# Dilated attention and gated recurrence: matmul order changed between two heads, and value transposes moved into the next product

## The chip, the cores and the metric

The kernel runs on one core of one Trainium2 chip. The metric is the device time of one execution in microseconds (us), from launch to end, as the median of several runs. Times inside an execution come from one profiled run and are counted from its first instruction.

## The reference, cut to what matters

The program is two transformer blocks on 512 positions of width 1024, in float32. The change touches two places of it.

The first place is the dilated attention of the first block. There are three branches (window 128 and dilation 1, 512 and 4, 2048 and 16) with 16 heads of 64 each:

```python
q = (h @ w_q).reshape(b, s, N_BRANCHES, N_HEADS, HEAD_DIM)
for g, (window, dil) in enumerate(BRANCHES):
    o, l = _dilated_branch(q[:, :, g], kv[:, :, 0, g], kv[:, :, 1, g], window, dil, slopes[g])
wts = jax.nn.softmax(jnp.stack(lses, axis=0), axis=0)
o = jnp.sum(wts[..., None] * jnp.stack(outs, axis=0).astype(jnp.float32), axis=0)
```

A branch computes scores of queries and keys, adds a distance bias with a causal band, takes a softmax, and multiplies by the values. Queries, keys and values are products of normalized activations with weight matrices.

The second place is the gated recurrence (HGRN) of the second block, in two layers, for a context of 256 positions and the 512 latent positions. Within blocks of 128 positions it needs masked products of decayed keys and queries, also with 64 channels for each head.

## The kernel before, in words

Activations lie transposed: 128 channels on the partitions, positions along the free axis. A weight tile of 128x1024 is loaded by DMA (`wprep`), and split by ScalarE and VectorE into a high and a low float32r part (L277, L281). A **product** (`acc`, `mm3`, L284 to L294) is then 8 steps over the contraction, each with three matmuls (L286, L287, L288) of 128x128 against 128x512, so 24 matmuls.

`dilated_attention` (L639) goes over 8 pairs of heads. A pair's two heads have 64 channels each and lie on partitions 0 to 63 and 64 to 127 of the same tiles. `project(p)` (L651) makes nine products for a pair, in the order k, v, q with three branches each. ScalarE evacuates each from PSUM (L672, L676, L678). A value product goes to a tile `vt`, of which there is one buffer. Four TensorE transposes (L686) follow at once into a PSUM tile `pv`, and ScalarE copies that to the tile `v` (L687), which has two buffers for each branch. Product outputs `pq` and transposes `pv` both come from the PSUM tag `a` (two buffers of one bank).

`attend(p)` (L690) makes the scores. For each head and each of two kinds (kind 0 is branch 0; kind 1 is branches 1 and 2 side by side) there is a score tile S of two PSUM banks from tag `b` (two buffers), filled in four steps u of 128 queries. A step is one matmul (L710 or L712) or two (L715, L716), with a contraction of 64 partitions. In float32 each is carried out as two passes, each with its own weight load. VectorE adds the bias and finds the row minimum (L719), and ScalarE takes the exponential (L720). GpSimd copies small rows about (L725, L726, L743), VectorE scales the probabilities (L755), TensorE transposes them (L758, to `pt`, tag `b`) and multiplies by the values (L774, to `po`). L774 alternates between the two heads, whose outputs lie on different partitions of `po`.

In the second block `hgrn_pair` calls `scores` (L1006), and this calls `products` (L1014) eight times: once for the diagonal and once for each of seven levels. A call has two heads times `nb` blocks (4 for the latent, 2 for the context) of matmuls with a contraction of 64 (L1020), one PSUM bank for each head. GpSimd, VectorE and ScalarE compute the next level's operands meanwhile (L1053 to L1064), and VectorE merges a result under a mask (L1030). The latent runs it for two pairs in each of two layers, 32 calls in all. The context has queries in the first layer alone, 16 calls.

The program is written with the Tile framework. It records the instructions with their dependencies and arranges each engine's stream at compile time: of the instructions whose inputs and buffers are ready in its own model, the one earliest in program order goes first. So matmuls of `project(p + 1)` stand between the scores of `attend(p)`. On the chip each stream runs in that order and waits on semaphores.

Of the kernel before, what the change touches and what calls it, by code (L numbers as in the profile page):

```python
# [11 lines left out]
F32 = mybir.dt.float32  # L12
F32R = mybir.dt.float32r
U8 = mybir.dt.uint8
AF = mybir.ActivationFunctionType
ALU = mybir.AluOpType
# [3 lines left out]
P = 128  # L20
D = 1024
DT = D // P
L = 512
# [615 lines left out]
def dilated_attention(K, pool, HK, seg, gates, done):  # L639
    nc = K.nc  # L640
    a = K.a
    H = seg.H
# [8 lines left out]
    def project(p):  # L651
        q, k, v = [None] * 3, [None] * 3, [None] * 3
        jobs = [(kind, b) for kind in "kvq" for b in range(3)]
        pre = {}
        if p == 0:
            outs = [[K.bank("pq")] for _ in range(3)]
            lead_in(K, [seg], outs, [a["wk"][b * 8] for b in range(3)], [HK])
            pre = {("k", b): outs[b][0] for b in range(3)}
        for kind, b in jobs:
            if (kind, b) in pre:  # L660
                ps = pre[(kind, b)]
            else:
                W = K.wprep(a["w" + kind][b * 8 + p])
                ps = K.bank("pq")
                K.acc(ps, W, H if kind == "q" else HK, slice(0, L))
            if kind == "v":
                t = pool.tile([P, L], F32, tag="vt", name="vt", bufs=1)
            else:
                t = pool.tile([P, L], F32, tag=f"{kind}{b}", name=f"{kind}{b}", bufs=2)
            if b:  # L670

                nc.scalar.activation(t.rearrange("p (r j) -> p r j", r=4), by_residue(ps), AF.Copy,  # L672
                                     scale=0.125 if kind == "q" else 1.0)
            elif kind == "q":

                nc.scalar.activation(halves(t), ps.rearrange("p (i j r) -> p i r j", i=4, r=4), AF.Copy, scale=0.125)  # L676
            else:
                nc.scalar.activation(t, ps, AF.Copy)  # L678
            if kind != "v":
                (q if kind == "q" else k)[b] = t  # L680
                continue

            v[b] = pool.tile([P, 4, P], F32, tag=f"v{b}", name=f"v{b}", bufs=2)
            pt = K.bank("pv").rearrange("p (u n) -> p u n", u=4)
            for u in range(4):
                nc.tensor.transpose(pt[:, u], t[:, P * u:P * u + P], K.ident)  # L686
            nc.scalar.activation(v[b], pt, AF.Copy)  # L687
        return q, k, v

    def attend(p, q, k, v):  # L690
        nm = pool.tile([P, 2, 2, 4], F32, tag="nm", name="nm", bufs=2)
        den = pool.tile([P, 2, 2, 4], F32, tag="den", name="den", bufs=2)
        probs = []
        for hh in range(2):
            rows = slice(64 * hh, 64 * hh + 64)
            bias = pool.tile([P, 2, 256], F32, tag="bias", name="bias", bufs=2)
            nc.sync.dma_start(bias.rearrange("p a b -> p (a b)"), a["bias"][2 * p + hh])
            pr = pool.tile([P, 8, 256], F32, tag="pr", name="pr", bufs=2)
            probs.append(pr)
            for kind in range(2):  # L700
                for u in range(4):
                    if u == 0:
                        S = K.bank("ps", "b").rearrange("p (u c) -> p u c", u=4)
                    cs = slice(0, 256)
                    Su = S[:, u]
                    qs = q[1 if kind else 0][rows, 128 * u:128 * u + 128]
                    if kind == 0:
                        if u == 0:
                            cs = slice(128, 256)
                            nc.tensor.matmul(Su[:, 128:256], qs, k[0][rows, 0:128], start=True, stop=True)  # L710
                        else:
                            nc.tensor.matmul(Su, qs, k[0][rows, 128 * u - 128:128 * u + 128], start=True, stop=True)  # L712
                    else:
                        q2 = q[2][rows, 128 * u:128 * u + 128]
                        nc.tensor.matmul(Su[:, 0:128], qs, k[1][rows, 128 * u:128 * u + 128], start=True, stop=True)  # L715
                        nc.tensor.matmul(Su[:, 128:256], q2, k[2][rows, 128 * u:128 * u + 128], start=True, stop=True)  # L716
                    o = pr[:, 4 * kind + u, cs]
                    m = nm[:, kind, hh, u:u + 1]
                    nc.vector.tensor_tensor_reduce(o, Su[:, cs], bias[:, kind, cs], -1.0, 3e38, ALU.add, ALU.min, m)  # L719
                    nc.scalar.activation(o, o, AF.Exp, bias=m, scale=-1.0, accum_out=den[:, kind, hh, u:u + 1])  # L720

        other = pool.tile([P, 2, 2, 4], F32, tag="other", name="other", bufs=2)
# [4 lines left out]
        m = pool.tile([P, 2, 4], F32, tag="mj", name="mj", bufs=2)  # L727
# [18 lines left out]
        for kind in range(2):  # L746
            for u0 in (0, 2):
                ps = K.bank("pt", "b").rearrange("p (u c h n) -> p u c h n", u=2, c=2, h=2)
                pt = pool.tile([P, 2, 2, 2, P], F32, tag="pt", name="pt", bufs=2)
# [51 lines left out]
class Mixer:  # L801
# [204 lines left out]
    def scores(self, pr, pool):  # L1006


        K, nc, nb, n = self.K, self.nc, self.nb, self.n
        C, D, X, Y = (self.hg[q, pr] for q in "CDXY")  # L1010
        queries = not self.only_state
        out = None

        def products(kt, qt, h):  # L1014
            S = K.bank("ph", "b").rearrange("p (h u c) -> p h u c", h=2, u=4)[:, :, :nb]
            for hh in range(2):
                rows = slice(64 * hh, 64 * hh + 64)
                for c in range(nb):
                    cs = slice(c * P, c * P + P)
                    nc.tensor.matmul(S[:, hh, c], kt[rows, cs], qt[rows, cs], start=True, stop=True)  # L1020
            if h == 0:
                nc.scalar.activation(out, S, AF.Copy)
            elif h >= 32:
                for b in range(128 // h):
                    r, c = slice(h * b, h * b + h), slice(h * (b ^ 1), h * (b ^ 1) + h)
                    nc.scalar.activation(out[r, :, :, c], S[r, :, :, c], AF.Copy)
            else:
                mk = self.lmask[:, LEVELS.index(h), None, :].to_broadcast([P, nb, P])
                for hh in range(2):
                    nc.vector.copy_predicated(out[:, hh], mk, S[:, hh])  # L1030

        if queries:
            qh = self.hg["qh", pr]
            out = pool.tile([P, 2, nb, P], F32, tag="at", name="at", bufs=1)
            ks = pool.tile([P, n], F32, tag="ka_", name="ka_", bufs=2)
            nc.gpsimd.tensor_tensor(ks, C, D, op=ALU.add)
            products(ks, qh, 0)
            Cq = pool.tile([P, n], F32, tag="qa_", name="qa_", bufs=2)
            Dq = pool.tile([P, n], F32, tag="qd_", name="qd_", bufs=1)
            nc.vector.tensor_tensor(Cq, qh, X, op=ALU.mult)  # L1040
            nc.vector.tensor_tensor(Dq, qh, Y, op=ALU.mult)
        for h in LEVELS[::-1]:
            if queries:
                products(C, Cq, h)
            m = 4 if h < 64 else 2
            outer, inner = (slice(0, 4, 3), slice(1, 3)) if m == 4 else (slice(0, 1), slice(1, 2))
            view = lambda t, w, hs: t.rearrange("p (g m h) -> p g m h", m=m, h=hs)[:, :, w]
            g = n // (m * h)
            each = lambda t, w: view(t, w, 1).to_broadcast([P, g, m // 2, h])

            def widen(eng, c, d, x, tag):
                r = pool.tile([P, n], F32, tag=tag, name=tag, bufs=2)
                eng.tensor_tensor(view(r, outer, h), view(c, outer, h), each(x, inner), op=ALU.mult)  # L1053
                nc.scalar.activation(view(r, inner, h), view(d, inner, h), AF.Copy)
                eng.tensor_tensor(view(d, inner, h), view(c, inner, h), each(x, outer), op=ALU.mult)
                return r

            C = widen(nc.gpsimd, C, D, X, "ka_")
            if queries:
                Cq = widen(nc.vector, Cq, Dq, Y, "qa_")  # L1060
            nX, nY = (pool.tile([P, n // (2 * h)], F32, tag=f"{t}{h}", name=t, bufs=1 if h < 64 else 2) for t in ("tx", "ty"))
            pairs = lambda t: t.rearrange("p (g m) -> p g m", m=m // 2)
            for t, p, q in ((nX, X, Y), (nY, Y, X)):
                nc.vector.tensor_tensor(pairs(t), view(p, outer, 1)[:, :, :, 0], view(q, inner, 1)[:, :, :, 0], op=ALU.mult)  # L1064
            X, Y = nX, nY
        return out, (C, D), (Dq, Cq) if queries else None, (Y, X)
# [598 lines left out]
```

## Time and profile before

| what | value |
|---|---|
| three runs | 3463.47, 3465.73, 3468.40 us; median 3465.73 |
| profiled execution | 3466.14 us, of which 3464.0 us between first and last instruction |
| TensorE matmuls busy | 3251.7 us (94%) |
| VectorE busy | 2192.0 us (63%) |
| ScalarE busy | 1439.6 us (42%) |
| GpSimd busy | 335.1 us (10%) |
| granted TensorE clock, mean | 0.98 |

How to read it: matmuls are pipelined and their ends are modelled, so a matmul's listed duration is longer than the distance to the next one's start. Distances between starts tell what a matmul costs. The attention of the first block runs from about 590 to 1210 us, the recurrence between 1630 and 1950 us (first layer) and between 2680 and 2830 us (second).

### The profile page before, as it was taken

How to read it: one execution, taken by the hardware profiler on the slowest of the kernel's cores; microseconds unless marked ns; L12 is line 12 of the kernel's file. 1: busy time of each engine (PE TensorE's matmuls, PEld its weight loads, DVE VectorE, ACT ScalarE, POOL GpSimd, SP SyncE). 2: the span in 40 equal slices, each digit the busy share in tenths (PEclk: the TensorE clock that was granted, in tenths of full speed). 3: DMA queues.
4: the chain of work that ended last, by engine and by line, in shares of the span. 5: the costliest groups of instructions: out<-in, count | busy, mean ns of one | idle time of the engine just before them, and what ended most of it. 6: DMA issues, size and time to landing. Idle time of an engine off the chain costs nothing.

```text
span 3464.0 us, 45725 instructions
## 1 busy us (share of the span) xinstructions
PE 3251.7 (94%) x17386; PEld 2692.3 (78%) x17386; DVE 2192.0 (63%) x3997; ACT 1439.6 (42%) x2680; POOL 335.1 (10%) x670
## 2 busy tenths in 40 slices
PE   4899998999999999999998999999999899999998
PEld 4677887777767778888887768888888787778887
DVE  7898646333333499946548888965446666675456
ACT  3342335334343443336535565322324644454333
POOL 3300001111111100002102101000000320000000
PEclk9999999999999999999999899999999989999999
DMA  6568422112121256522122114541122210132232
GB/s 235 191 237 311 145 94 87 70 54 93 66 75 67 74 179 205 194 91 104 53 84 83 40 56 145 199 172 58 60 72 81 68 35 31 51 107 98 97 98 80
DMA packets 125075, 375.57 MB, mean 108 GB/s; under 512 B 14004, under 2 KB 27060, under 8 KB 124856
## 3 DMA queue, kind: packets, MB, share of 16 engines
q1 hardware_dynamic: 124856, 372.65, 31.6%
q8 instruction: 137, 2.24, 0.3%
q14 instruction: 82, 0.67, 0.1%
HBM read 365.25 MB, written 7.35 MB: 108 GB/s over the span
## 4 chain that ended last, share of the span: by engine, by line
PE 42%; DVE 6%; ACT 2%; issue 2%; POOL 1%; DMA 0%; POOLq 0%; ACTq 0%; DVEq 0%
PE pu L287 5%; PE pu L288 4%; PE pu L286 4%; PE pd L286 3%; PE pd L287 3%; PE pd L288 3%; PE pS L1212 2%; PE pj L287 1%; PE pj L286 1%; PE pj L288 1%; PE pc L288 1%; PE pc L287 1%; PE pc L286 1%; PE pO L1231 1%; PE pv L902 1%
## 5 line engine op out<-in xcount | busy, mean ns | idle before, releaser
L277 ACT ACTIVATE wh<-wr 128x1024 fp32r<-128x1024 f32 (+5 forms) x521 | 488.4, 938 | 1045.4 <-PE pd L287 299.3
L281 DVE TENSOR_TENSOR wl<-wr,wh 128x1024 fp32r<-128x1024 f32 (+5 forms) x501 | 539.1, 1076 | 605.2 <-ACT wh L277 601.3
L286 PE MATMUL pu<-h_512h,wh 128*128 128x512 f32 (+1 forms) x1472 | 562.5, 382 | 7.4 <-ACT h_512h L390 6.6
L287 PE MATMUL pu<-h_512l,wh 128*128 128x512 f32 (+1 forms) x1472 | 564.4, 383 | 3.0 <-POOL h_512l L395 2.6
L288 PE MATMUL pu<-h_512h,wl 128*128 128x512 f32 (+1 forms) x1472 | 561.6, 381 | 0.0
L286 PEld LDWEIGHTS pu<-h_512h,wh 128*128 128x128 f32 x1472 | 279.5, 190 | 59.8 <-ACT h_512h L390 7.7
L287 PEld LDWEIGHTS pu<-h_512l,wh 128*128 128x128 f32 x1472 | 279.3, 190 | 57.7 <-POOL h_512l L395 4.9
L288 PEld LDWEIGHTS pu<-h_512h,wl 128*128 128x128 f32 x1472 | 279.4, 190 | 52.8
L286 PE MATMUL pd<-g_512h,wh 128*128 128x512 f32 x656 | 256.4, 392 | 4.5 <-DVE x L399 4.2
L287 PE MATMUL pd<-g_512l,wh 128*128 128x512 f32 x656 | 255.6, 390 | 0.0
L288 PE MATMUL pd<-g_512h,wl 128*128 128x512 f32 x656 | 255.2, 389 | 0.0
L399 DVE SCALAR_TENSOR_TENSOR x<-pd,mod,x 128x512 f32<-128x512 f32 x162 | 121.1, 748 | 167.9 <-PE pd L288 167.1
L310 DVE CUSTOM_DVE_ANT_0 ada<-ada,row_c 128x1024 f32<-128x1024 f32 x144 | 185.7, 1298 | 28.2 <-DMA ada<-in_ada 24.9
L286 PEld LDWEIGHTS pd<-g_512h,wh 128*128 128x128 f32 x656 | 123.0, 188 | 33.0 <-issue 4.6
L288 PEld LDWEIGHTS pd<-g_512h,wl 128*128 128x128 f32 x656 | 123.2, 188 | 25.7
L287 PEld LDWEIGHTS pd<-g_512l,wh 128*128 128x128 f32 x656 | 123.3, 188 | 25.1 <-DVE g_512l L298 0.8
L522 ACT ACTIVATE ca<-ca 128x512 f32<-128x512 f32 (+1 forms) x110 | 64.1, 583 | 127.9 <-DVE ca L511 119.2
L287 PE MATMUL pj<-h_512l,wh 128*128 128x512 f32 (+1 forms) x280 | 107.6, 385 | 3.1 <-POOL h_512l L395 2.5
L286 PE MATMUL pj<-h_512h,wh 128*128 128x512 f32 (+1 forms) x280 | 106.0, 382 | 2.7 <-ACT h_512h L390 2.0
L288 PE MATMUL pj<-h_512h,wl 128*128 128x512 f32 (+1 forms) x280 | 106.6, 382 | 1.2 <-DVE wl L281 1.2
L281 POOL TENSOR_TENSOR wl<-wr,wh 128x1024 fp32r<-128x1024 f32 (+1 forms) x20 | 47.8, 2392 | 567.5 <-ACT wh L277 543.8
L288 PE MATMUL pc<-h_256h,wl 128*128 128x256 f32 x352 | 99.6, 283 | 0.0
(1152 smaller groups left out, 7464.6 us busy)
## 6 DMA issues: line engine op xcount, KB each, us to landing
ada<-in_ada SPq DMA_DIRECT2D x192, 512.0 KB, 4.6
wr<-in_up SPq DMA_DIRECT2D x88, 512.0 KB, 3.7
wr<-in_bup SPq DMA_DIRECT2D x88, 512.0 KB, 3.5
wr<-in_in SPq DMA_DIRECT2D x36, 512.0 KB, 3.4
wr<-in_wk SPq DMA_DIRECT2D x24, 512.0 KB, 3.5
wr<-in_wv SPq DMA_DIRECT2D x24, 512.0 KB, 3.5
wr<-in_wq SPq DMA_DIRECT2D x24, 512.0 KB, 3.5
wr<-in_out SPq DMA_DIRECT2D x48, 256.0 KB, 2.6
```

The source lines that it names most:

```text
L277: nc.scalar.activation(hi[:, :n], r[:, :n], AF.Copy)
L281: (eng or nc.vector).tensor_tensor(lo[:, :n], r[:, :n], hi[:, :n], op=ALU.subtract)
L286: mm(ps, whi, hhi, start=first, stop=False)
L287: mm(ps, whi, hlo, start=False, stop=False)
L288: mm(ps, wlo, hhi, start=False, stop=last)
L310: nc.vector.tensor_tensor_reduce(o, r, cond, 1.0, 0.0, ALU.mult, ALU.add, mod[:, t:t + 1])
L399: self.nc.vector.scalar_tensor_tensor(x, ps, gate, x, op0=ALU.mult, op1=ALU.add)
L522: K.last_silu = nc.scalar.activation(ca, ca, AF.Silu)
L902: nc.tensor.matmul(ps, hh[:, s], w[0][:, ws], start=kt == 0, stop=False)
L1212: nc.tensor.matmul(S[:, o:o + m], self.q[h][rows, qs], kt[rows, :], start=True, stop=True)
L1231: nc.tensor.matmul(O[:, qb % 2 * P:qb % 2 * P + P], vals[kb], at[:, kb * P:kb * P + P], start=qb % 2 == 0 and kb == 0, stop=qb % 2 == 1 an ...
```

## The change

Three edits. In `project`, a value product is evacuated directly into the tile `v`. Its transposes are kept back until the first half (contraction steps 0 to 3) of the next product has been issued; they go to `pv` and are copied back over `v` in place. In `attend`, the loop over heads moves inward: both heads' S tiles of a kind are open together, and matmuls alternate between the heads. In `products`, the loop over heads moves inside the loop over blocks.

```diff
+        def to_tokens(b):
+            pt = K.bank("pv").rearrange("p (u n) -> p u n", u=4)
+            for u in range(4):
+                nc.tensor.transpose(pt[:, u], v[b][:, u], K.ident)
+            nc.scalar.activation(v[b], pt, AF.Copy)
...
-                K.acc(ps, W, H if kind == "q" else HK, slice(0, L))
-            if kind == "v":
-                t = pool.tile([P, L], F32, tag="vt", name="vt", bufs=1)
+                K.acc(ps, W, H if kind == "q" else HK, slice(0, L), range(4))
+                if turn is not None:
+                    to_tokens(turn)
+                    turn = None
+                K.acc(ps, W, H if kind == "q" else HK, slice(0, L), range(4, 8))
...
+            if kind == "v":
+                v[b] = t.rearrange("p (u n) -> p u n", u=4)
+                turn = b
...
+        for kind in range(2):
+            S = [K.bank("ps", "b").rearrange("p (u c) -> p u c", u=4) for _ in range(2)]
+            for u in range(4):
+                us = slice(128 * u, 128 * u + 128)
+                cs = slice(128 if kind == 0 and u == 0 else 0, 256)
+                if kind:
+                    parts = [(slice(0, 128), q[1], k[1], us), (slice(128, 256), q[2], k[2], us)]
+                else:
+                    parts = [(cs, q[0], k[0], slice(max(128 * u - 128, 0), 128 * u + 128))]
+                for to, qt, kt, ks in parts:
+                    for hh in range(2):
+                        rows = slice(64 * hh, 64 * hh + 64)
+                        nc.tensor.matmul(S[hh][:, u, to], qt[rows, us], kt[rows, ks], start=True, stop=True)
+                for hh in range(2):
+                    o = probs[hh][:, 4 * kind + u, cs]
...
         def products(kt, qt, h):
-            for hh in range(2):
-                rows = slice(64 * hh, 64 * hh + 64)
-                for c in range(nb):
-                    cs = slice(c * P, c * P + P)
+            for c in range(nb):
+                cs = slice(c * P, c * P + P)
+                for hh in range(2):
+                    rows = slice(64 * hh, 64 * hh + 64)
                     nc.tensor.matmul(S[:, hh, c], kt[rows, cs], qt[rows, cs], start=True, stop=True)
```

## Rows read from the trace of the kernel before

**Rows 1.** The page: busy time by engine; the chain that ended last, by engine.
```profile
PE 3251.7 (94%) x17386; PEld 2692.3 (78%) x17386; DVE 2192.0 (63%) x3997; ACT 1439.6 (42%) x2680; POOL 335.1 (10%) x670
PE 42%; DVE 6%; ACT 2%; issue 2%; POOL 1%; DMA 0%; POOLq 0%; ACTq 0%; DVEq 0%
```

**Rows 2.** Busy time by stretch: attention, recurrence of first and second layer.
```profile
core 0: us, PE busy (x) PEld busy (x) DVE busy (x) ACT busy (x) POOL busy (x), PEclk, DMA share, GB/s
690.00:760.00 70.00, 64.05 (x341) 48.44 (x339) 22.94 (x66) 27.96 (x58) 9.04 (x48) 1.00 0.17 60
1860.00:1900.00 40.00, 34.62 (x219) 27.73 (x219) 38.78 (x94) 20.10 (x44) 17.32 (x18) 0.91 0.14 52
2785.00:2820.00 35.00, 32.04 (x213) 27.23 (x213) 27.98 (x57) 17.59 (x40) 12.12 (x15) 0.85 0.11 38
```

**Rows 3.** Waits in 600 to 1180 us: who waited for whom, total, times, longest.
```profile
PE pv L686 <- ACT vt L672: 21.1, 15, 1.4
```

**Rows 4.** Instructions on tile pv: duration min/median/max, first and last start.
```profile
L687 ACT ACTIVATE v<-pv x24: 597/598/600, 587.7 to 1157.1; 128x512 f32<-128x512 f32 x24
```

**Rows 5.** Timeline, 28 matmuls of products in a row: start, duration, what.
```profile
689.92 0.39 PE L287 MATMUL pq<-h_512l,wh 128*128 128x512 f32 x1
...
696.26 0.39 PE L288 MATMUL pq<-h_512h,wl 128*128 128x512 f32 x1
```

**Rows 6.** Timeline at the end of a value product.
```profile
662.71 0.39 PE L288 MATMUL pq<-hk7h,wl 128*128 128x512 f32 x1
662.91 1.06 ACT L277 ACTIVATE wh<-wr 128x1024 fp32r<-128x1024 f32 x1 [3.89 <-PE pq L287]
663.87 0.58 ACT L678 ACTIVATE vt<-pq 128x512 f32<-128x512 f32 x1
664.51 0.66 PE L686 MATMUL pv<-mats,vt 128*128 128x128 f32 x4 [1.41 <-ACT vt L678]
```

**Rows 7.** Timeline, transposes inside a product with their input at hand.
```profile
715.73 0.48 PE L287 MATMUL pq<-hk1l,wh 128*128 128x512 f32 x1
716.05 0.92 PE L758 MATMUL pt<-mats,pr 128*128 128x128 f32 x7
```

**Rows 8.** Windows, instructions on pq alone, score phases of two pairs (PE, PEld, ...).
```profile
696.58:710.70 14.12, 6.46 (x17) 2.76 (x16) 0.58 (x1) 1.00 0.16 56
783.68:798.43 14.75, 6.79 (x20) 3.36 (x21) 0.00 (x0) 1.00 0.44 155
```

**Rows 9.** Timeline of a score step in steady state, and visits of one tile alone.
```profile
701.98 0.70 PE L712 MATMUL ps<-k,q 64*128 64x256 f32 x2
702.51 0.38 PE L715 MATMUL ps<-k,q 64*128 64x128 f32 x2
702.71 0.42 DVE L719 CUSTOM_DVE_ANT_0 pr<-ps,bias 128x256 f32<-128x256 f32 x1 [0.63 <-PE ps L712]
702.73 0.38 PE L716 MATMUL ps<-k,q 64*128 64x128 f32 x2
703.05 0.50 PE L288 MATMUL pq<-hk2h,wl 128*128 128x512 f32 x1
703.15 0.43 DVE L719 CUSTOM_DVE_ANT_0 pr<-ps,bias 128x256 f32<-128x256 f32 x1
703.48 0.49 PE L710 MATMUL ps<-k,q 64*128 64x128 f32 x2
703.89 0.51 PE L286 MATMUL pq<-hk3h,wh 128*128 128x512 f32 x1
...
710.09 0.48 PE L715 MATMUL ps<-k,q 64*128 64x128 f32 x2
710.41 0.38 PE L716 MATMUL ps<-k,q 64*128 64x128 f32 x2
710.72 0.50 PE L287 MATMUL pq<-hk5l,wh 128*128 128x512 f32 x1
```

**Rows 10.** Timeline, a visit that holds scores of both heads.
```profile
704.33 0.37 PE L715 MATMUL ps<-k,q 64*128 64x128 f32 x1
704.36 0.48 PE L712 MATMUL ps<-k,q 64*128 64x256 f32 x1
...
704.98 0.50 PE L287 MATMUL pq<-hk3l,wh 128*128 128x512 f32 x1
```

**Rows 11.** Timeline, value products that alternate between the heads.
```profile
719.89 2.03 PE L774 MATMUL po<-pt,v 128*64 128x128 f32 x32
721.85 1.09 PE L758 MATMUL pt<-mats,pr 128*128 128x128 f32 x8
```

**Rows 12.** Timeline, one call of products, latent and context.
```profile
1658.89 0.72 PE L1020 MATMUL ph<-qa__13133,ka__13129 64*128 64x128 f32 x8 [0.21 <-DVE qa__13133 L1053]
1659.55 0.39 PE L287 MATMUL pj<-h_256l,wh 128*128 128x256 f32 x1
...
1876.05 1.71 PE L1020 MATMUL ph<-qa__15556,ka__15552 64*128 64x128 f32 x16
1877.69 0.50 PE L287 MATMUL pj<-h_512l,wh 128*128 128x512 f32 x1
```

**Rows 13.** Windows (as rows 2), a stretch at a lower granted clock.
```profile
1940.00:1950.00 10.00, 10.00 (x38) 6.50 (x37) 5.31 (x11) 0.92 (x2) 0.06 (x1) 0.55 0.15 54
```

**Rows 14.** Chain of waits: one matmul of a product at the low clock.
```profile
1906.87 0.43 PE pj L288
```

More of the change, by code (lines that the diff above doesn't have):

```diff
@@ L664, in project @@
                 ps = K.bank("pq")
-                K.acc(ps, W, H if kind == "q" else HK, slice(0, L))
-            if kind == "v":
-                t = pool.tile([P, L], F32, tag="vt", name="vt", bufs=1)
-            else:
-                t = pool.tile([P, L], F32, tag=f"{kind}{b}", name=f"{kind}{b}", bufs=2)
+                K.acc(ps, W, H if kind == "q" else HK, slice(0, L), range(4))
+                if turn is not None:
+                    to_tokens(turn)
+                    turn = None
+                K.acc(ps, W, H if kind == "q" else HK, slice(0, L), range(4, 8))
+            t = pool.tile([P, L], F32, tag=f"{kind}{b}", name=f"{kind}{b}", bufs=2)
             if b:
@@ L678, in project @@
                 nc.scalar.activation(t, ps, AF.Copy)
-            if kind != "v":
+            if kind == "v":
+                v[b] = t.rearrange("p (u n) -> p u n", u=4)
+                turn = b
+            else:
                 (q if kind == "q" else k)[b] = t
[L681 to L687, printed above, removed]
         return q, k, v
@@ L692, in attend @@
         den = pool.tile([P, 2, 2, 4], F32, tag="den", name="den", bufs=2)
-        probs = []
+        biases, probs = [], []
         for hh in range(2):
-            rows = slice(64 * hh, 64 * hh + 64)
[L696 to L717, printed above, removed]
@@ new lines, in attend @@
+            biases.append(pool.tile([P, 2, 256], F32, tag="bias", name="bias", bufs=2))
+            nc.sync.dma_start(biases[hh].rearrange("p a b -> p (a b)"), a["bias"][2 * p + hh])
+            probs.append(pool.tile([P, 8, 256], F32, tag="pr", name="pr", bufs=2))
+        for kind in range(2):
[5 more added lines that the diff above has]
+                    parts = [(slice(0, 128), q[1], k[1], us), (slice(128, 256), q[2], k[2], us)]
+                else:
+                    parts = [(cs, q[0], k[0], slice(max(128 * u - 128, 0), 128 * u + 128))]
[5 more added lines that the diff above has]
+                    o = probs[hh][:, 4 * kind + u, cs]
@@ L718, in attend @@
                     m = nm[:, kind, hh, u:u + 1]
-                    nc.vector.tensor_tensor_reduce(o, Su[:, cs], bias[:, kind, cs], -1.0, 3e38, ALU.add, ALU.min, m)
+                    nc.vector.tensor_tensor_reduce(o, S[hh][:, u, cs], biases[hh][:, kind, cs], -1.0, 3e38,
+                                                   ALU.add, ALU.min, m)
                     nc.scalar.activation(o, o, AF.Exp, bias=m, scale=-1.0, accum_out=den[:, kind, hh, u:u + 1])
@@ L1015, in products @@
             S = K.bank("ph", "b").rearrange("p (h u c) -> p h u c", h=2, u=4)[:, :, :nb]
-            for hh in range(2):
-                rows = slice(64 * hh, 64 * hh + 64)
-                for c in range(nb):
-                    cs = slice(c * P, c * P + P)
+            for c in range(nb):
+                cs = slice(c * P, c * P + P)
+                for hh in range(2):
+                    rows = slice(64 * hh, 64 * hh + 64)
                     nc.tensor.matmul(S[:, hh, c], kt[rows, cs], qt[rows, cs], start=True, stop=True)
```

## The prediction

> **What bounds the kernel now.** I read the page first. TensorE's matmuls are busy 94% of the span, VectorE 63%, and the chain that ended last lies on PE by far the most [rows 1]. A busy PE can hide waits, so I then read the stages by windows. In the attention, 70 us hold 64 us of PE against 23 us of VectorE and 28 us of ScalarE, all at the full granted clock [rows 2]. TensorE alone sets that stage, and its time there counts one for one. In the recurrence VectorE takes 38.8 of 40 us in the first layer; in the second it takes 28.0 of 35 and PE 32.0 [rows 2]. There a shorter matmul counts in part.
>
> The list of waits then shows what TensorE waits for in the attention: transposes L686 for the evacuation of `vt` [rows 3]. The timeline gives the price. A product's matmuls start 6.34/28 = 0.226 us apart [rows 5]. The last one of a value product starts at 662.71; ScalarE first ends a weight split (1.06 us), then evacuates (0.58 us), and the transposes start at 664.51 [rows 6]: 1.80 us for a matmul worth 0.226.
>
> **Edit A, transposes inside the next product.** There are 24 of them (24 copies L687 [rows 4]), three for each of eight pairs. Now 12 matmuls of the next product follow at once, 12 x 0.226 = 2.7 us. The evacuation ended about 664.45, 1.74 us after the last matmul started [rows 6], so it fits with 1 us to spare. Breaking into a product where the input is at hand costs 0.32 us from the matmul before to the first transpose (715.73 to 716.05) [rows 7]. So 1.80 - 0.32 = 1.48 us goes, 24 times: **35.5 us**. The transposes and both ScalarE copies stay as many as before, and the way back from transposes to a product is walked once each time, before and after. No DMA moves past another: weight loads keep their order on SP's queue.
>
> What is late next? Three things could be. The copy of `pv` over `v` must end before the product after next needs the bank; it has the other 12 matmuls, 2.7 us, for 0.60 us of work [rows 4]. Weight splits, 1.06 us of ScalarE for each product [rows 6], have 24 x 0.226 = 5.4 us. The wait now stands in the middle of a product, and behind it in TensorE's stream stands that product's second half; nobody waits for that but its own evacuation. If the cover went altogether, the wait would be back, a gain of 0. The other end is 24 x (1.80 - 0.226) = 38 us, with no break at all. I take 35.5, because rows 6 and 7 are both direct measurements.
>
> **Edit B, scores alternate between heads.** The score phase of the pair at 696.58 lasts 14.12 us and holds 16 matmuls of products (17 less the one still in flight at its start) [rows 8]. These are worth 3.6 us, so the scores cost 10.5 us of TensorE. The phase of 14.75 us holds 20: 10.2 us. I take 10.3.
>
> A steady step runs from 701.98 to 703.48, 1.50 us: score matmuls of two S tiles 1.07 us (to 703.05), one matmul of a product, and two changes between 64 and 128 rows; of the 0.43 us from 703.05 to 703.48 the product is worth 0.226, so a change costs about 0.2 [rows 9]. The two S tiles are kind 0 and kind 1 of one head, on the same 64 partitions, so their passes queue up. One visit shows the alternative by chance: L715 of one head and L712 of the other start 0.03 us apart, and the visit, with six passes like the other, lasts 704.33 to 704.98, 0.65 us instead of 1.07 [rows 10]. So both halves of the array work at once, and 0.42 us of each step could go.
>
> Not all of it will. The next step of a tile starts only after VectorE has read the last one. With both heads started at s, VectorE begins 0.73 us later (701.98 to 702.71) and takes 0.44 us for each (702.71 to 703.15) [rows 9], so the first head's next step may start at s + 1.2 and the second's at s + 1.6. If the stream still holds one product matmul for each step, the steps alternate between about 1.2 (TensorE then waits for the second head) and 1.46 us (the second head, being late, leaves less to wait for): a mean of 1.33 instead of 1.50. Eight steps, the first a short one of 0.41 (703.48 to 703.89 [rows 9]) and a change of 0.2: 0.62 + 7 x (1.33 - 0.226) = 8.35 us for a pair, against 10.3. The last pair has no project behind it and its chain goes over VectorE and GpSimd, so I count seven pairs: 7 x 1.95 = **14 us**. The ends are in the rivals: 26 us gained, 18 us lost. I take the value nearest to rows 9, where VectorE's pace and the static order are those measured.
>
> By the Trainium skill (TensorEngine Tiling (Array Packing), Theoretical Speedup), a contraction of 64 or less may run up to 2 times as fast. Rows 10 bear out that the two halves run together; the sum by that rule is the second rival below.
>
> **Edit C, recurrence.** A latent call takes 1.64 us (1876.05 to 1877.69) for 16 passes [rows 12]. Head after head already overlaps a little. Where matmuls alternate, 32 passes take 1.96 us [rows 11], 0.055 for each beside a change of 0.2; 16 would take 0.88 + 0.2 = 1.1 us, a gain of 0.55. The context's call of 8 passes takes 0.66 us [rows 12] and would take 0.64: nothing. So 32 x 0.55 = 18 us of TensorE. In the first layer VectorE is full and hides it; I let a fifth through, 2 us. In the second PE and VectorE share the bound; I let half through, 4 us. Together **6 us**, bounds 0 and 18.
>
> **Sum.** 35.5 + 14 + 6 = 55.5 us off the profiled execution's own 3466.1 us gives 3410.6. That execution lay 0.4 us above the median of the runs, so 3410. Its own range is 3397 to 3426 (A 33 to 37, B 7 to 20, C 0 to 12).
>
> **Rivals.**
> - *Split steps, 3442.* VectorE frees the heads 0.44 us apart, so the compile-time order could put a product's matmul between them. Each head then comes alone: a short visit takes 0.41 us (703.48 to 703.89) and a full one of four passes 0.63 (710.09 to 710.72) [rows 9], so a pair's 16 visits with their changes cost 2 x 0.41 + 14 x 0.63 + 16 x 0.2 = 12.9 us, 2.6 more than 10.3: 7 x 2.6 = 18 us lost, 35.5 + 6 - 18 = 24 gained. Against it: two tiles freed the same 0.44 us apart already stand in one visit in rows 9.
> - *Full overlap, 3398.* With more product matmuls in each step VectorE never holds TensorE: 0.41 + 7 x 0.65 + 8 x 0.2 = 6.6 us a pair, 7 x 3.7 = 26 us; 35.5 + 26 + 6 = 67.5. For it: rows 10. Against: the order must change.
> - *The bank, 3446.* `pq` and `pv` share two buffers. If these were handed out in turn, each product after a value product would wait for the evacuation of the one before, and A would be 0: 14 + 6 = 20 gained. Against: in the second block's attention one tile holds one of two buffers while four transposes go through the other (L1223 to L1228), which handing out in turn would not allow.
> - *The clock, 3485, slower.* The stretch at 1940 has PE busy all 10 us at a granted clock of 0.55, near the lower level of 1.2 GHz [rows 13], and it is full of matmuls of 64 rows and transposes; a product's matmul then takes 0.43 us [rows 14]. If twice as dense work on 64 rows drew the clock down in the score phases, a pair would lose 16 x 0.2 = 3.3 us on products and about 4 on scores, and some 2 us more until the clock is back: 9.4 x 8 = 75 us, 55.5 - 75 = -20. It decides from 55.5/8 = 7 us a pair. Against: the clock is at full in the attention now, through idle times and scores [rows 2].
>
> **How the numbers follow.** The forecast 0.57, full overlap 0.14, split steps 0.13, the bank 0.06, the clock 0.07, and 0.03 for several small losses that cancel. The range 3388 to 3448 takes in the first two, the split and most of the bank, and a larger part of C. A measurement here can tell 0.2%, 7 us, from no change. Faster 0.90, same 0.03, slower 0.07.
>
> **What would show it.** A: no wait of L686 for an evacuation, 0.32 us from a product's matmul to the first transpose, in its middle. B: steps of about 1.33 us, both heads' matmuls a few hundredths apart or with a short wait for VectorE; visits of 0.64 us that hold one head alone would show the split. C: calls of 1.1 us, and more idle PE around them in the first layer. The prediction is wrong if products wait at their start, if the clock falls below 1.00 between 600 and 1180 us, or if the stage before 1180 us shrinks by less than 40 us.

## The result, and the profile after

| | before | after |
|---|---|---|
| median (range) of four runs each | 3465.59 us (3463.47 to 3468.40) | 3407.58 us (3404.39 to 3412.42) |
| profiled execution, span | 3466.14, 3464.0 us | 3404.39, 3402.3 us |

The ratio is 0.984, 95% interval 0.982 to 0.986: 58 us faster, at 3408 us against 3410 forecast. First the page of the changed kernel, busy time by engine as in [rows 1]; then one row of windows for each stage, of before and then of after: the attention (from its first matmul to the first of the next part) and the latent's recurrence in the second layer (from its first to its last `ph` matmul). Columns as in [rows 2].

```profile
PE 3206.1 (94%) x17386; PEld 2659.6 (78%) x17386; DVE 2186.9 (64%) x3997; ACT 1436.4 (42%) x2680; POOL 338.3 (10%) x670
```

```profile
556.20:1226.90 670.70, 614.76 (x3246) 476.28 (x3246) 261.28 (x685) 274.76 (x576) 84.79 (x394) 0.99 0.21 73
...
2758.70:2829.30 70.60, 62.32 (x440) 53.92 (x440) 55.59 (x120) 31.97 (x72) 25.47 (x31) 0.85 0.08 27
```

```profile
556.50:1177.40 620.90, 591.59 (x3246) 465.67 (x3246) 257.35 (x685) 272.93 (x576) 84.55 (x394) 0.99 0.23 78
...
2702.90:2767.60 64.70, 52.71 (x438) 43.99 (x439) 55.50 (x120) 31.69 (x72) 26.43 (x31) 0.87 0.09 30
```

With the same instructions, attention is 49.8 us shorter and the second layer 5.9. The latent's recurrence in the first layer (its row stands under edit C) is 8.0 us shorter. That makes 63.7; the stretches between give 2.0 back, and the spans differ by 61.7.

**Edit A in the trace.** The timeline around a value product, to be laid beside [rows 6]:

```profile
655.29 0.39 PE L288 MATMUL pq<-hk7h,wl 128*128 128x512 f32 x1
655.49 1.06 ACT L277 ACTIVATE wh<-wr 128x1024 fp32r<-128x1024 f32 x1 [3.90 <-PE pq L287]
655.51 0.39 PE L286 MATMUL pq<-hk0h,wh 128*128 128x512 f32 x1
...
656.45 0.58 ACT L689 ACTIVATE v<-pq 128x512 f32<-128x512 f32 x1
...
658.01 0.40 PE L288 MATMUL pq<-hk3h,wl 128*128 128x512 f32 x1
658.24 0.60 PE L665 MATMUL pv<-mats,v 128*128 128x128 f32 x4
658.60 0.48 PE L286 MATMUL pq<-hk4h,wh 128*128 128x512 f32 x1
658.94 0.60 ACT L666 ACTIVATE v<-pv 128x512 f32<-128x512 f32 x1 [1.91 <-PE pv L665]
```

The product ends at 655.29 and the next one follows 0.22 us later. ScalarE still splits first and evacuates then (to 657.03), and TensorE does not notice. The transposes begin 0.23 us after a product's matmul (1.80 in [rows 6]) and the product goes on 0.36 us after that. No wait of L665 is left in the list of waits.

**Edit B in the trace.** Score steps in steady state, as in [rows 9]; PEld is the weight load ahead of the first matmul:

```profile
689.72 0.68 PEld L718 LDWEIGHTS ps<-k,q 64*128 64x128 f32 x8 [0.25 <-DVE nm L722]
689.72 0.87 PE L718 MATMUL ps<-k,q 64*128 64x128 f32 x8
...
690.47 0.42 DVE L722 CUSTOM_DVE_ANT_0 pr<-ps,bias 128x256 f32<-128x256 f32 x1 [0.64 <-PE ps L718]
690.52 0.50 PE L288 MATMUL pq<-hk2h,wl 128*128 128x512 f32 x1
690.82 0.42 DVE L722 CUSTOM_DVE_ANT_0 pr<-ps,bias 128x256 f32<-128x256 f32 x1
...
690.96 1.05 PE L718 MATMUL ps<-k,q 64*128 64x128 f32 x8
...
692.37 0.88 PE L718 MATMUL ps<-k,q 64*128 64x128 f32 x8
...
693.61 0.37 PE L718 MATMUL ps<-k,q 64*128 64x128 f32 x1
```

Steps start 1.24, 1.41 and 1.24 us apart. The first one shown waits 0.25 us for VectorE's reading of the step before it, with one product matmul between. Between 595 and 1210 us, all visits of TensorE to the scores (from the first score matmul to the next other one, and the extra distance ahead of it) cost 80.0 us before, in 82 visits, and 63.5 after, in 66: 16.5 us saved. Five pairs went from 10.3 to 7.7 us, the last from 9.4 to 7.9; the other two, with 9.7 and 9.5 us the cheapest of the first seven before, only to 8.6.

Something came back. The list of waits, 600 to 1130 us, of before and of after:

```profile
PE pt L758 <- DVE pr L755: 9.8, 7, 1.7
```

```profile
PEld ps L718 <- DVE nm L722: 16.7, 55, 0.4
...
PE pt L762 <- DVE pr L759: 15.4, 7, 2.4
```

The lines on `pt` are TensorE standing before a pair's first probability transpose until VectorE has scaled the probabilities: 5.6 us more after, in seven pairs. (The line on `ps` sums 55 waits like the one shown above, 0.30 us on average.) Both heads' scores now end together, and the chain behind them (GpSimd's copies, the factors, the scaling) is longer: in five pairs the first probability transpose came 4.4 us after the last score before and 5.1 to 5.2 us after the change, with 11 matmuls of products beside the chain in both.

A second thing came with this wait. For the seventh pair, the first row of each fence is TensorE's wait, from the start of the matmul ahead of it, and the second is a stretch just behind; before, then after, with the granted clock in the column PEclk:

```profile
1113.70:1115.72 2.02, 0.39 (x3) 0.00 (x1) 1.54 (x11) 1.17 (x2) 0.85 (x5) 1.00 0.05 19
1117.80:1121.20 3.40, 3.39 (x37) 2.56 (x37) 3.01 (x8) 2.04 (x3) 1.40 (x7) 1.00 0.00 0
```

```profile
1066.58:1069.33 2.75, 0.39 (x2) 0.03 (x1) 1.72 (x12) 0.21 (x1) 1.40 (x9) 1.00 0.18 68
1070.70:1074.10 3.40, 3.40 (x21) 2.08 (x20) 3.01 (x10) 1.07 (x3) 1.88 (x10) 0.50 0.02 5
```

After the longer wait the granted clock fell to half (0.50). In this profile it does so behind two of the seven waits, and the pattern runs through all 14 profiles of this case. Before, five of the seven distances from a product's matmul to the first probability transpose are about 2.0 us; after, five are 2.7 to 2.8. The six profiles without edit B have the shorter waits and no time at half clock between 600 and 1160 us. The eight with it have the longer ones and two to four stretches at half clock each, eight in the kernel with the longest waits (3.9 to 4.3 us). All but one of these stretches begin 2.5 to 5.1 us after the matmul ahead of such a wait started.

**Edit C in the trace.** A latent call, beside the second pair of [rows 12], and then the latent's recurrence in the first layer from its first to its last `ph` matmul, before and after:

```profile
1824.21 1.16 PE L1024 MATMUL ph<-qa__15532,ka__15528 64*128 64x128 f32 x16
1825.30 0.50 PE L287 MATMUL pj<-h_512l,wh 128*128 128x512 f32 x1
```

```profile
1862.70:1951.60 88.90, 80.04 (x474) 63.85 (x474) 77.42 (x161) 37.03 (x81) 31.80 (x34) 0.85 0.13 47
```

```profile
1813.20:1894.10 80.90, 66.26 (x474) 52.09 (x474) 76.89 (x161) 36.96 (x81) 32.06 (x34) 0.92 0.15 51
```

The call takes 1.09 us instead of 1.64. Not every call shows this, as some wait for operands and some run at half clock: all visits of TensorE to `ph` sum to 37.0 us instead of 41.1 in the first layer and to 31.6 instead of 39.4 in the second. In the first layer, VectorE has 77 us of work in both; what differs beside TensorE's work is the granted clock, 0.85 and 0.92. Whether the 8 us are the edit's or the clock's is asked below.

### The profile page after: what moved, and what is told of

Read it like the earlier page. It is cut to its first block, busy times and chain, and to the rows that moved or that the text cites. A ratio compares the mean times of both kernels' runs of the same rounds, so it can differ in the third digit from the quotient of the medians.

```text
span 3402.3 us, 45745 instructions
## 1 busy us (share of the span) xinstructions
PE 3206.1 (94%) x17386; PEld 2659.6 (78%) x17386; DVE 2186.9 (64%) x3997; ACT 1436.4 (42%) x2680; POOL 338.3 (10%) x670
## 4 chain that ended last, share of the span: by engine, by line
PE 41%; DVE 7%; ACT 2%; issue 2%; DMA 1%; POOL 1%; SPq 0%; POOLq 0%; ACTq 0%; DVEq 0%
PE pu L287 5%; PE pu L286 5%; PE pu L288 5%; PE pd L286 3%; PE pd L287 3%; PE pd L288 3%; PE pS L1216 2%; PE pj L286 1%; PE pj L287 1%; PE pj L288 1%; PE pc L288 1%; PE pc L287 1%; PE pc L286 1%; PE pO L1235 1%; PE pv L906 1%
```

## The experiments

### Each edit by itself

Edit A alone: `project` from the changed kernel, `attend` and `products` from the one before.

```diff
...
-                K.acc(ps, W, H if kind == "q" else HK, slice(0, L))
...
+                K.acc(ps, W, H if kind == "q" else HK, slice(0, L), range(4))
+                if turn is not None:
+                    to_tokens(turn)
+                    turn = None
+                K.acc(ps, W, H if kind == "q" else HK, slice(0, L), range(4, 8))
...
```

> The kernel before with the first edit alone: value transposes in place, half a product later. Theory (TensorE stood still for the evacuation, 1.57 us for each of 24 value products): 35 to 38 us faster than before, 3428 to 3431, all of it between 600 and 1180 us, and no wait of a transpose. Rival (the wait moves to the start of the product after, which needs the shared bank): no more than 7 us faster.

Measured: 3421.59 us, ratio 0.987 (0.985 to 0.989). Attention 629.6 us against 670.7, 41 us less, so A is the main part; another 7 us went in the first layer's recurrence, which A does not touch (see the last experiment).

Edit B alone: `attend` from the changed kernel.

```diff
-        for hh in range(2):
...
-            for kind in range(2):
-                for u in range(4):
...
+        for kind in range(2):
...
+            for u in range(4):
...
+                for to, qt, kt, ks in parts:
+                    for hh in range(2):
...
```

> The kernel before with the second edit alone: scores of the dilated attention alternate between two heads. Theory (both halves of the array work at once, VectorE's reading of the tile sets the step): steps of 1.24 to 1.40 us instead of 1.50, 14 to 17 us faster, 3449 to 3452. Rival (the steps gain only because the first edit keeps products ready beside them): under 7 us faster. Rival (steps split): slower by some 18 us.

Measured: 3453.57 us, ratio 0.997 (0.996 to 0.998), 11 us, less than the 14 to 17 expected. Attention is 6.7 us shorter. The visits cost what they cost in the changed kernel, 16.5 us less than before, but the distances from a product's matmul to the probability transposes sum to 25.3 us, before 18.0. The saving in the scores is real and nearly half of it comes back as that wait. Of the 9.2 us left, 2.5 more are missing; the stage has 22.4 us at half clock in this profile, 11.9 before, and 10.5 us more at half speed are worth up to 5 us.

Edit C alone: `products` from the changed kernel.

```diff
-            for hh in range(2):
...
-                for c in range(nb):
...
+            for c in range(nb):
...
+                for hh in range(2):
...
```

> The kernel before with the third edit alone: the recurrence's products alternate between two heads. Theory (a latent call takes 1.1 instead of 1.64 us, 32 calls, and more of it gets through than the 6 us predicted, since the profile after shows 8 us in the first layer and 6 in the second): 10 to 14 us faster. Rival (these stretches start at another moment after the first two edits and meet their loads and transfers differently): 2 to 6 us.

Measured: 3460.13 us, ratio 0.998 (0.997 to 1.000), 6 us; the theory's 10 to 14 did not come. The latent's recurrence in both layers of this kernel, in windows as above:

```profile
1861.90:1951.10 89.20, 71.87 (x474) 55.24 (x474) 77.13 (x161) 36.58 (x80) 31.85 (x33) 0.87 0.14 46
...
2760.40:2825.00 64.60, 51.06 (x439) 42.60 (x439) 55.60 (x120) 31.85 (x72) 25.65 (x31) 0.89 0.09 30
```

In the second layer 64.6 us, as in the changed kernel (before: 70.6). In the first layer TensorE is busy 8.2 us less and the stage is as long as before; VectorE has its 77 us there. That VectorE hides the gain is argued, not shown. Over all 14 profiles the second layer took 64.4 to 65.2 us with the edit and 70.3 to 70.6 without. C is worth 6 us in the second layer and, by the last experiment, about 1 at most in the first.

### Why the wait of edit A was there

The kernel before with the value evacuated into `v`, which has two buffers, and the transposes in place but directly behind the product:

```diff
-                t = pool.tile([P, L], F32, tag="vt", name="vt", bufs=1)
+                t = pool.tile([P, L], F32, tag=f"v{b}", name=f"v{b}", bufs=2)
...
-            v[b] = pool.tile([P, 4, P], F32, tag=f"v{b}", name=f"v{b}", bufs=2)
+            v[b] = t.rearrange("p (u n) -> p u n", u=4)
```

> The kernel before with value products evacuated into the two-buffered tile and transposed in place, but at once, as before. Theory (the gain is the matmuls that cover the evacuation): no change, within 7 us of before, and the transposes start 1.80 us after the last matmul. Rival (the single buffer of the old tile held the evacuation up): most of the 35 us gained.

Measured: 3462.55 us, ratio 0.999 (0.998 to 1.001); the gap from the last matmul of a value product to its transposes is still 1.79 us. The single `vt` was not the reason, and the work in place by itself brings nothing.

The changed kernel, with the transposes placed after one contraction step of the next product instead of four:

```diff
-                K.acc(ps, W, H if kind == "q" else HK, slice(0, L), range(4))
+                K.acc(ps, W, H if kind == "q" else HK, slice(0, L), range(1))
...
-                K.acc(ps, W, H if kind == "q" else HK, slice(0, L), range(4, 8))
+                K.acc(ps, W, H if kind == "q" else HK, slice(0, L), range(1, 8))
```

> The changed kernel, but a value product's transposes stand after the first of the next product's eight contraction steps (3 matmuls, 0.68 us) instead of the fourth. Theory (the matmuls in between are the cover of an evacuation that ends some 1.7 us after the last matmul): each of 24 transposes again waits, about 1.80 - 0.23 - 0.68 = 0.9 us, so 21 us slower than the changed kernel, about 3429. Rival (any place inside the next product will do, since the bank or the buffer was what held TensorE): within 7 us of the changed kernel.

Measured: 3408.01 us, ratio 0.984 (0.983 to 0.985): no slower than the changed kernel, so 3429 did not come. In the timeline seven matmuls stand between the product and the transposes, though the source puts three there:

```profile
652.84 0.39 PE L288 MATMUL pq<-hk7h,wl 128*128 128x512 f32 x1
653.07 0.39 PE L286 MATMUL pq<-hk0h,wh 128*128 128x512 f32 x1
...
654.42 0.39 PE L286 MATMUL pq<-hk2h,wh 128*128 128x512 f32 x1
654.65 0.64 PE L665 MATMUL pv<-mats,v 128*128 128x128 f32 x4
```

The compile-time order moves ready matmuls ahead of transposes whose input is late. Then why not in the kernel before? There the product being evacuated holds one of the two banks of tag `a`, and `pv`, asked for ahead of the next `pq`, the other; the next product had no bank to start in. Two runs test that. The first is the kernel before with one word changed, `pv` from another tag:

```diff
-            pt = K.bank("pv").rearrange("p (u n) -> p u n", u=4)
+            pt = K.bank("pv", "s").rearrange("p (u n) -> p u n", u=4)
```

> The kernel before, with one thing changed: the transposed value product is allocated from the third kind of PSUM bank (two of them, used otherwise by the output product and the sums) instead of from the two banks that the value products themselves come from. Transposes are written where they were, directly behind the product, into a copy, with one vt buffer. Theory (it was the turn of the two banks that kept the next product's matmuls behind the transposes, and once the turn is free they are put ahead of them): the gap from the last matmul of a value product to its transposes falls from 1.80 to about 0.23 us, attention is 35 to 42 us shorter, the whole 3421 to 3430 us, which is what the projection edit alone gave. Rival (the place inside the next product that the source gives the transposes is what covers the evacuation): gap stays 1.80, whole time within 5 us of 3463 to 3466.

Measured: 3423.62 us, ratio 0.988 (0.986 to 0.990); attention 631.7 us, 2 us more than with edit A alone. Around a value product:

```profile
660.71 0.39 PE L288 MATMUL pq<-hk7h,wl 128*128 128x512 f32 x1
...
661.88 0.58 ACT L672 ACTIVATE vt<-pq 128x512 f32<-128x512 f32 x1
...
662.30 0.39 PE L286 MATMUL pq<-hk2h,wh 128*128 128x512 f32 x1
662.53 0.64 PE L686 MATMUL pv<-mats,vt 128*128 128x128 f32 x4
```

The gap is 0.23 us with seven matmuls ahead, in 23 of the 24 products (1.55 in the first), and nothing else of edit A is in this kernel. The bank was the reason. The second run is the changed kernel with the order forced: three matmuls, the transposes, then the rest.

```diff
-                K.acc(ps, W, H if kind == "q" else HK, slice(0, L), range(4))
+                K.acc(ps, W, H if kind == "q" else HK, slice(0, L), range(1))
+                pin = nullcontext()
                 if turn is not None:
-                    to_tokens(turn)
+                    pin = K.tc.issue_after(to_tokens(turn).ins)
                     turn = None
-                K.acc(ps, W, H if kind == "q" else HK, slice(0, L), range(4, 8))
+                with pin:
+                    K.acc(ps, W, H if kind == "q" else HK, slice(0, L), range(1, 8))
...
```

> The changed kernel, with the transposes held in front: the next product gives three matmuls, then the four transposes, and its other 21 matmuls are ordered behind them. Theory (TensorE stands until the evacuation of the value product is done, and each matmul put ahead of the transposes takes 0.227 us of that wait): the gap from last matmul of the product to first transpose is 1.80 us as before, with three matmuls in it, so 1.80 minus 3 x 0.227 = 1.1 us, less 0.23 for one ordinary step, are waited, about 0.9 us x 24 = 21 us: whole time 3425 to 3433 us. Rival (what cost the time was not the evacuation but the change itself between the product's matmuls and fp32 transposes): no difference, within 4 us of the changed kernel's 3405 to 3410.

Measured: 3433.98 us (3427.04 to 3447.31), ratio 0.992 (0.989 to 0.994); the median is 1 us above the expected range. Attention is 644.4 us, 23.5 more than in the changed kernel. The gap is 1.12 us in 23 of the 24 products (1.78 in the first):

```profile
665.08 0.39 PE L288 MATMUL pq<-hk0h,wl 128*128 128x512 f32 x1
665.57 0.58 ACT L685 ACTIVATE v<-pq 128x512 f32<-128x512 f32 x1
...
666.20 0.66 PE L665 MATMUL pv<-mats,v 128*128 128x128 f32 x4 [0.73 <-ACT v L685]
```

So the wait is for the evacuation, and each matmul ahead of the transposes takes its 0.227 us off it: 1.80 with none, 1.12 with three, 0.23 with seven.

### Must the matmuls alternate finely, and is more to be had?

The changed kernel with the loop over heads outside that over the parts, so that inside a step one head follows the other:

```diff
-                for to, qt, kt, ks in parts:
-                    for hh in range(2):
-                        rows = slice(64 * hh, 64 * hh + 64)
+                for hh in range(2):
+                    rows = slice(64 * hh, 64 * hh + 64)
+                    for to, qt, kt, ks in parts:
...
```

> The changed kernel, but inside a score step of kind 1 both matmuls of one head come before both of the other, instead of alternating matmul by matmul. Theory (the array takes up the other half's passes a few instructions ahead, and VectorE's reading sets the step): within 5 us of the changed kernel. Rival (halves work together only where neighbours in the stream alternate): kind 1 steps go back to 1.5 us, 7 to 10 us slower.

Measured: 3408.48 us, ratio 0.984 (0.983 to 0.986), visits 63.5 us: the same. But this does not show that the order inside a step is without effect. In all 66 visits the passes signal the other engines in the same sequence as in the changed kernel, and in 62 they start at the same distances to 0.012 us (between the two executions of the changed kernel, in 63). So the compile-time order was probably the same in both, whatever the source says, and the question is open.

One S tile for each step, with both heads in it, so that the next step does not wait for VectorE's reading of the last:

```diff
-            S = [K.bank("ps", "b").rearrange("p (u c) -> p u c", u=4) for _ in range(2)]
             for u in range(4):
+                S = K.bank("ps", "b").rearrange("p (h c) -> p h c", h=2)
...
-                        nc.tensor.matmul(S[hh][:, u, to], qt[rows, us], kt[rows, ks], start=True, stop=True)
+                        nc.tensor.matmul(S[:, hh, to], qt[rows, us], kt[rows, ks], start=True, stop=True)
...
```

> The changed kernel with one score tile for each step, both heads in a bank each, two buffers, instead of one tile for each head and kind. So a step's matmuls wait for VectorE's reading of the step before last, not of the last one. Theory (VectorE's reading holds the steps at 1.24 to 1.40 us): the wait of score matmuls for VectorE, 16.7 us in all now, goes, steps near 1.1 us, 6 to 12 us faster than the changed kernel, unless the probability transposes, which already wait for VectorE, wait longer by the same amount. Rival (the next wait takes it all): within 4 us.

Measured: 3410.88 us (3408.11 to 3419.11), ratio 0.985 (0.984 to 0.987): no gain. The visits did shrink, to 34 and 44.6 us (63.5). The wait took most of that:

```profile
PE pt L762 <- DVE pr L759: 26.8, 7, 3.9
```

The distances to the probability transposes sum to 36.5 us against 23.6, 12.9 of the 18.9 won. The profiled execution also had more of the stage at half clock, 44.9 us against 16.7; 28.2 us more at half speed are worth up to 14 us. This execution was the slowest of its four, but all four had a lower mean granted clock (0.972 to 0.978) than the changed kernel's four (0.979 to 0.982), so the clock has a part in the median as well. Here the wait at the probability transposes was the longest, 3.9 to 4.3 us of distance, and a stretch at half clock stands behind each of the seven.

The same alternation in the scores of the second block's attention (L1212 of the changed kernel):

```diff
-            for c in range(2):
...
-                S = K.bank("pS", "b")
...
-                for kt, m in keys:
-                    nc.tensor.matmul(S[:, o:o + m], self.q[h][rows, qs], kt[rows, :], start=True, stop=True)
-                    o += m
+            SS = [K.bank("pS", "b") for _ in range(2)]
...
+            for kt, m in keys:
+                for c in range(2):
...
+                    nc.tensor.matmul(SS[c][:, o:o + m], self.q[h][rows, qs], kt[rows, :], start=True, stop=True)
+                o += m
...
```

> The changed kernel, and the same alternation in the second block's attention, whose two score halves lie on partitions 0 to 63 and 64 to 127 as well. A latent query block has 8 passes, 4 of 512 and 4 of 256 columns, about 2.6 us head after head. Theory (halves run together): 1.3 us less for each of 32 latent query blocks, 41 us of TensorE; VectorE and ScalarE take part of it back, so 10 to 35 us faster than the changed kernel. Rival (that stage waits for its softmax, not for its scores): within 5 us.

Measured: 3416.65 us, ratio 0.987 (0.985 to 0.988): 9 us slower than the changed kernel, which neither theory said. The first layer's attention kept its length. The second's, from the end of the recurrence to the last score, in the changed kernel, in this one, and in the one with a tile for each step:

```profile
2767.60:2967.70 200.10, 194.96 (x1125) 153.00 (x1123) 124.60 (x220) 94.31 (x200) 13.87 (x8) 1.00 0.13 44
```

```profile
2768.00:2979.70 211.70, 206.74 (x1144) 159.94 (x1144) 128.54 (x223) 94.42 (x201) 14.36 (x8) 0.97 0.14 44
```

```profile
2775.80:2982.20 206.40, 201.29 (x1125) 156.95 (x1124) 124.60 (x220) 94.47 (x200) 13.88 (x8) 0.97 0.13 42
```

The third kernel has this stage unchanged and is 6.3 us longer there at the same 0.97. So about half of the 11.6 us may be the clock; the rest comes with the edit, and why is open. Nor did the run test its theory: in the second layer 15 of the 128 score passes start within 0.05 us of the pass before, in this kernel as in the changed one, and the visits to these scores cost 42.2 us against 40.1. (In the first block's attention, edit B took that count from 10 to 81 of 384 passes.) The alternation stands in the source, and TensorE's stream hardly shows it; what kept the halves apart is not shown.

### The first layer's 8 us

Both kernels once more, unchanged, for a second profile of each.

> The kernel before, once more, for its profile. Theory (the 7 us that the changed kernel wins in the recurrence of the first block is time at half clock, which differs from one execution to the next and has no part in the edits): the time at half clock between 1830 and 1980 us is another one than the 30.6 us of the first profile, by 3 to 20 us, and the length of the recurrence differs by half of that. Rival (the half-clock stretches are fixed by the program): 30.6 us again, within 2, and the same recurrence length within 1 us.

> The changed kernel, once more, for its profile. Theory (half-clock time of the first block's recurrence differs from execution to execution): another one than the 13.6 us of the first profile, up to 30 us, and the recurrence longer by half of the difference. Rival (fixed by the program): 13.6 us within 2, the recurrence 7 to 8 us shorter than before's again.

Measured: 3469.59 and 3410.17 us. The first layer, before and after:

```profile
1863.10:1953.50 90.40, 80.14 (x474) 63.90 (x474) 77.56 (x161) 36.95 (x81) 31.60 (x34) 0.85 0.14 46
```

```profile
1812.90:1900.90 88.00, 71.09 (x474) 54.94 (x474) 77.47 (x161) 37.19 (x81) 32.47 (x34) 0.86 0.15 47
```

The changed kernel takes 80.9 us in one execution and 88.0 in the other, at 0.92 and 0.86. The kernel before came out alike twice in clock (27.3 us at half in the stage both times) and 1.5 us apart in length; in the wider window of the expectation, 30.7 and 27.3 us. So for that kernel neither theory nor rival fits; in the changed kernel 10.2 us more at half clock go with 7.1 us more length, where the theory had half. Over all 14 profiles the stage took 80.9 to 83.2 us where at most 20.5 us of it lay at half clock, and 87.0 to 90.5 where 23.9 or more did. Edit C does not sort them: edit A alone (82.1 us, clock 0.92) is among the short ones, and C alone (89.2) among the long. At equal time at half clock, the profiles with and without edit C lie close: 80.9 us with all edits and 82.1 with A alone, at 13.7 us each; 82.9 with the early transposes and 83.2 with B alone, at 17.1. So up to 8 us of a measured difference there go with the clock of an execution, and about 1 with edit C. All four profiles with the attention's waits as before lie among the long ones; of the ten with a shorter attention six are short. Whether a shorter attention shifts these odds is open.

## Why the prediction was right, and where by luck

**Edit A**: 35.5 us forecast. By the median gaps, with the way back to the product, (1.796 + 0.41) before less (0.23 + 0.355) after, 1.62 x 24 = 38.9 us. The term that was off is the break into a product, taken as 0.32 us from [rows 7]. It measured 0.23, an ordinary step. In the rows, a transpose stands right ahead of the matmul that the 0.32 us are counted from:

```profile
715.71 0.27 PE L758 MATMUL pt<-mats,pr 128*128 128x128 f32 x1
715.73 0.48 PE L287 MATMUL pq<-hk1l,wh 128*128 128x512 f32 x1
```

So part of that transpose's time was taken for a price of the break; each of the 14 distances of 0.32 us in the trace of before has one 0.02 to 0.09 us ahead. For the rest, the reason given was half of it: the cover is as said, 1.8 us of evacuation behind matmuls, but the place of the transposes in the source does not make it. The bank did, as `pv` in another tag showed. The rival "the bank" looked for this in the kernel after; it stood in the one before.

**Edit B**: 14 us forecast. Its steps came as worked out (1.24 and 1.41 us against 1.2 and 1.46), with VectorE's reading as the limit, and the visits gave 16.5 us over eight pairs. The term that was mis-sized is what comes late next: the longer wait for the scaled probabilities, counted as nothing, measured 5.6 us. The cost of a pair was also forecast too high, 8.35 us against 7.7 in five pairs, while the two pairs that were cheap before gained about 1 us each instead of 1.95. B is worth about 11 us in the attention: 38.9 + 16.5 - 5.6 = 49.8, and the stage shrank by 49.8. That match is closer than the terms are known: by themselves, A took 41 us off the stage and B 6.7, and the clock's 2 us are in neither sum.

**Edit C**: 6 us forecast, 4 of them in the second layer and 2 in the first; 6 and about 1 at most measured. A call with its operands at hand came out at 1.09 us against 1.1. The visits fell by 12 us in all, against 18 forecast. Of TensorE's 9.6 us less in the second layer, 5.9 went through.

**The rivals.** Split steps and full overlap did not come; the steps alternate as forecast. The clock came, small: in the attention the granted clock fell below 1.00, which the prediction had named as a sign that it would be wrong. 16.7 us lay at half speed instead of 11.9 (23.5 in the second profile, with a stage of 624.3 us, 3.4 longer for 6.8 more at half). That is 2 to 6 us, not 75. Nor did it come where the rival put it, in the score phases with their dense work on 64 rows: it fell behind the wait for the probabilities, which edit B made longer. The profiles sort by that wait; no run changed the wait alone, so that it is the cause is not shown. The rival's 2 us until the clock is back rest on no row; a stretch of 3.4 us at half clock costs up to 1.7.

**The sum**: 49.8 + 6 = 55.8 us from the edits against 55.5 forecast. A was 3 too small and B 3 too large, so part of that closeness is luck. The other 6 us between the two profiled executions are the first layer's 8.0, most of which go with the clock, less the 2.0 given back between the stages.

## What to carry to other kernels

Where TensorE waits for an evacuation, look at what holds the next work's buffer: an order made at compile time fills the wait by itself as soon as the next product can have a bank, so ask for that bank first or take the short-lived tile from another tag. Where two heads use half the rows each, have both open in one step, and read from the trace whether their passes do run together: in the first block's attention they did, in the second block's the same edit to the source hardly changed TensorE's order. And price what waits behind a sped-up step: a third to two thirds of what the scores won came back at the next chain over VectorE, and the longer wait there brought time at half clock with it.

## What the runs showed of the hardware that was not expected

- Going from a product's matmuls to fp32 transposes with their input at hand costs no more than one ordinary step, 0.23 us (658.01 to 658.24 in the timeline under edit A).
- In the attention the granted clock fell to half just behind TensorE's waits for the probabilities, in all eight profiles with edit B and its longer waits (2.7 to 2.8 us in most pairs) and in none of the six without (about 2.0 us).
- The time at half clock in one and the same stage of one and the same kernel was 13.7 us in one execution and 23.9 in the next, and the stage 80.9 and 88.0 us. A difference of 7 us in that stage can't be read from one profile of each kernel.
- A stage that ran at a full clock in twelve profiles (200.0 to 200.2 us) ran at 0.97 in two, for 206.4 us in a kernel that leaves it unchanged.
